# The low part of the attention weights in two GpSimd instructions of 256 columns in a hybrid decoder layer

## The chip, the cores and the metric

One core of a Trainium2 chip. The metric is the time of the kernel on the device in microseconds, median of the runs; less is better. Engines are named as in the profile: PE is TensorE's matmul, PEld its weight load, DVE VectorE, ACT ScalarE, POOL GpSimd, SP the engine that issues the DMAs.

## The reference

A decoder layer on x of 2048 tokens and 1024 channels. The input projection feeds a sparse attention of 8 heads (head dim 64, shared keys and values) and a gated short convolution; then an output projection, a DeepNorm, a SwiGLU FFN of width 2816 and a second DeepNorm. What matters here is the attention: for each query an indexer picks 256 keys, and softmax weights over these multiply the shared values.

```python
logits = jnp.einsum('bqhd,bqkd->bhqk', q_b, kg).astype(jnp.float32) * attn_scale
logits = jnp.where(valid[:, None], logits, NEG_INF)
p = jax.nn.softmax(logits, axis=-1).astype(v.dtype)
return jnp.einsum('bhqk,bqkd->bqhd', p, vg)
```

## The kernel before, in words

The sequence is cut into 16 blocks of 128 queries and 16 tiles of 128 keys. No keys are gathered: a mask `u` per query block holds 0 for a chosen key and a large negative number for the others, and the logits of all keys up to the block get it added. float32 products are made from fp16 pairs: a matrix is split into a high part (its fp16 copy) and a low part (the rest), and three of the four products are summed in PSUM.

The attention goes over the blocks in the order `ORDER`, and in each block over its key tiles, one step per pair of block and key tile, 136 steps in all.

- `weigh` (L881 to L898) makes the weights of a step, in two tiles of 4 heads (128 keys x 512 columns of head and query). Three matmuls make the logits: L888 queries and keys, L889 the mask, L890 minus the row's maximum. ACT takes the exponential into `p32` in float32 (L894) and copies it to fp16 as `ph` (L895). GpSimd subtracts the two, `pr = p32 - ph`, the low part in fp16 (L896). So L896 runs 272 times. `p32` has 5 buffers, `ph` and `pr` have 6 each.
- `values` (L900 to L908) runs `LAG` = 2 steps later. For each of 8 heads it multiplies 128 columns of `ph` with the values' high and low part (L906, L907) and 128 columns of `pr` with the high part (L908), all into one accumulator per block. One `pr` tile serves 4 matmuls of L908, one per 128 columns.
- `finish` (L910 to L923) copies the accumulator to SBUF (L912) and takes squares and sums for the head norm on DVE (L915, L917, L918, L922); `root` (L786 to L798) makes a reciprocal root with ACT and four small DVE operations (L795 to L798).
- `maxima` (L856 to L879) makes the row maxima of later blocks: matmuls of L863, a DVE reduction of each with the mask (L865), and at the end a small product on GpSimd (L878).
- `mix` (L925 onward) is the output projection (L946), residual, norm (L950 to L956) and transposes (L964) of a finished block.
- Beside this, `background` runs the top-k search of the late blocks (11 to 15): counting passes on ACT and DVE (L512, L514) and many small DVE operations on 2 to 12 columns that move the bracket (L517 to L546), then L555 to L564. When they are done, GpSimd, ACT and DVE make the first weights and inputs of the FFN (L215, L216, L1092 to L1111, L1169, L1170).

Which instruction comes when on each engine's queue is not the program's order alone. The kernel is traced in a tile framework, opened as `TileContext(nc, schedule_with_timeline_sim=True)`: it orders the instructions of each engine by their priorities and by a timeline that it works out before the run, and it sets the semaphores. Work on maxima is pulled forward by `tc.high_priority(offset=MXP)` with MXP = 400. On the chip each engine runs its queue in that fixed order.

Of the kernel before, what the change touches and what calls it, by code (L numbers as in the profile page):

```python
# [16 lines left out]
ALU = mybir.AluOpType  # L17
# [10 lines left out]
CH = 512  # L28
# [114 lines left out]
def body(ctx: ExitStack, tc: tile.TileContext, A, out, force=False):  # L143
    nc = tc.nc
    V, S_, G, T = nc.vector, nc.scalar, nc.gpsimd, nc.tensor
# [675 lines left out]
    def attention(pool=None, background=None, at_block=None, at_end=None):  # L821
# [60 lines left out]
        def weigh(b, kt, qst, q2, u):  # L882
            ksl = slice(kt * P, (kt + 1) * P)
            parts = []
            for g in range(2):
                hs = slice(g * 4, g * 4 + 4)
                pl_ = psa.tile([P, CH], F32, tag="l", name="l", bufs=LB)
                T.matmul(pl_, k1T[:, ksl], qst[:, hs], start=True, stop=False)  # L888
                T.matmul(pl_, u[:, ksl], i4, start=False, stop=False)  # L889
                T.matmul(pl_, k2T[:, ksl], q2[:, hs], start=False, stop=True)  # L890
                p32 = aq[0].tile([P, CH], F32, tag="p32", name="p32", bufs=pb_)
                ph = aq[0].tile([P, CH], F16, tag="ph", name="ph", bufs=2 * lag + 2)
                pr = aq[0].tile([P, CH], F16, tag="pr", name="pr", bufs=2 * lag + 2)
                S_.activation(p32, pl_, AF.Exp, scale=DH ** -0.5)  # L894
                S_.activation(ph, p32, AF.Copy)  # L895
                G.tensor_tensor(pr, p32, ph, op=ALU.subtract)  # L896
                parts.append((ph, pr))
            return parts  # L898

# [116 lines left out]
        for i in range(len(steps) + lag):  # L1016
            if i < len(steps):
                p, b, kt = steps[i]
                left = b - kt
                if kt == 0:  # L1020
                    while mixes and mixes[0][2] <= p - keep:
                        advance(mixes.pop(0), 999)
                    if look or p:
                        peak(p + look)
                    urgent(peaks.pop(p), 999)
                    if at_block is not None:
                        at_block(p)
                    mc = ap.tile([P, 4, 2, P], F16, tag="mc", name=f"mc{b}", bufs=keep)
                    dma(mc, m_d[b // 4][:, b % 4])
                    x = ap.tile([P, D], F32, tag="x", name=f"x{b}", bufs=keep)  # L1030
                    dma(x, A["x"][b * P:(b + 1) * P])
                    outs_[p] = x, mc
                tiles_[i] = weigh(b, kt, *held[p])
# [600 lines left out]
```

## Time and profile before

| | |
|---|---|
| median of 3 runs | 2590.02 us (2584.93 to 2590.75) |
| profiled execution, its own time | 2585.36 us |
| its span | 2583.5 us |
| PE busy | 2335.9 us |
| DVE busy | 1835.4 us |
| ACT busy | 1185.9 us |
| POOL busy | 1184.6 us |
| mean granted clock of TensorE | 0.956 |

The profile is one execution; times inside it are microseconds from the start of the span. Durations of single instructions are in nanoseconds. A view by stretches gives each engine's busy time in each stretch; a view by groups puts instructions of one line, operation and shape together with their mean duration and the idle time of the engine in front of them; a view of one line gives its shortest, median and longest duration; the timeline gives start and duration of each instruction.

### The profile page before, as it was taken

What the parts mean: (1) busy time and instruction counts of PE and PEld (TensorE: products, weight loads), DVE (VectorE), ACT (ScalarE), POOL (GpSimd) and SP (SyncE); (2) the same over time, 40 slices, a digit from 0 to 9 for tenths busy, and PEclk for the clock granted to TensorE, in tenths of its full rate; (3) what the DMA queues carried; (4) which work ended last, traced back from release to release, by engine and by line L of the source; (5) the groups of instructions that cost most, each with busy time, mean ns of one, the idle gap of its engine ahead of it and who ended that gap; (6) DMA issues with size and microseconds to landing.
All of it is one profiled execution on the core that took longest, in us unless ns stands there. A gap on an engine that the chain in (4) does not pass through costs nothing. (4 is left out here: it accounts for less than half of the span.)

```text
span 2583.5 us, 38131 instructions
## 1 busy us (share of the span) xinstructions
PE 2335.9 (90%) x13538; PEld 1126.0 (44%) x13538; DVE 1835.4 (71%) x3649; ACT 1185.9 (46%) x2263; POOL 1184.6 (46%) x960
## 2 busy tenths in 40 slices
PE   6799999996878799889969999999999996999998
PEld 3444444443444355445524444444444442444443
DVE  8998999989999877774377676666666687422223
ACT  3687776546766556667643333233323343110000
POOL 3000000004444655786555665565555664855445
PEclk8899999997988899999989999999999997999999
DMA  7321442433131422331233222222223236444443
GB/s 267 130 101 68 144 136 89 161 132 111 59 108 49 145 80 71 106 115 45 84 116 102 90 86 74 76 72 78 86 75 88 87 106 200 149 138 149 131 134 123
DMA packets 213913, 281.69 MB, mean 109 GB/s; under 512 B 15824, under 2 KB 128848, under 8 KB 212944
## 3 DMA queue, kind: packets, MB, share of 16 engines
q1 hardware_dynamic: 213712, 279.17, 33.9%
q8 instruction: 107, 1.75, 0.3%
q14 instruction: 94, 0.77, 0.1%
HBM read 183.20 MB, written 95.91 MB: 108 GB/s over the span
## 5 line engine op out<-in xcount | busy, mean ns | idle before, releaser
L1206 PE MATMUL f<-h,wwg 128*128 128x512 f16 x1800 | 418.8, 383 | 26.5 <-ACT h L1169 19.9
L896 POOL TENSOR_TENSOR pr<-p,ph 128x512 f16<-128x512 f32 x272 | 330.8, 1233 | 218.1 <-ACT ph L895 160.4
L1206 PE MATMUL f<-h,wwu 128*128 128x512 f16 x1800 | 413.5, 379 | 0.0
L1502 PEld LDWEIGHTS <-gi 128*128 128x128 f16 x1848 | 181.5, 99 | 276.1 <-DMA gi<-gg_d 44.8
L1240 POOL TENSOR_TENSOR go<-g,go 128x512 f16<-128x512 f32 x126 | 169.6, 1356 | 275.2 <-ACT go L1239 235.1
L1206 PEld LDWEIGHTS <-wwu 128*128 128x128 f16 x1848 | 180.8, 98 | 234.4 <-issue 17.3
L1206 PEld LDWEIGHTS <-wwg 128*128 128x128 f16 x1848 | 181.8, 99 | 232.0 <-issue 14.1
L1502 PE MATMUL f<-wdo,gi 128*128 128x512 f16 x1032 | 241.9, 387 | 14.9 <-DMA gi<-gg_d 6.9
L865 DVE CUSTOM_DVE_ANT_0 jk<-m,ua 128x512 bf16<-128x512 f32 (+3 forms) x320 | 193.7, 605 | 71.9 <-PE m L863 56.1
L894 ACT ACTIVATE p<-l 128x512 f32<-128x512 f32 x272 | 157.3, 596 | 91.1 <-PE l L890 82.6
L1239 ACT ACTIVATE go<-g 128x512 f16<-128x512 f32 x132 | 82.4, 627 | 230.7 <-issue 82.8
L447 ACT ACTIVATE r<-xs 128x512 f32<-128x512 f32 (+3 forms) x304 | 153.5, 547 | 59.2 <-PE xs L446 15.4
L895 ACT ACTIVATE ph<-p 128x512 f16<-128x512 f32 x272 | 166.1, 632 | 3.9 <-PE o L908 0.8
L1502 PE MATMUL f<-wdr,gi 128*128 128x512 f16 x576 | 136.8, 386 | 16.7 <-DVE g L1213 8.8
L737 PE MATMUL b<-hi,wch 128*128 128x512 f16 x384 | 146.8, 382 | 0.0
L737 PE MATMUL b<-lo,wch 128*128 128x512 f16 x384 | 146.6, 382 | 0.0
L737 PE MATMUL b<-hi,wcl 128*128 128x512 f16 x384 | 146.3, 381 | 0.0
L908 PE MATMUL o<-vst,pr 128*128 128x65 f16 x1088 | 136.1, 197 | 9.3 <-POOL pr L896 9.1
L906 PE MATMUL o<-vst,ph 128*128 128x65 f16 x1088 | 138.7, 195 | 3.1 <-ACT ph L895 2.0
L863 PE MATMUL m<-k1T,qst 128*128 128x512 f16 (+3 forms) x320 | 109.2, 372 | 35.6 <-DVE mp L865 31.5
L907 PE MATMUL o<-vst,ph 128*128 128x64 f16 x1088 | 138.5, 195 | 0.0
L1469 ACT ACTIVATE frs<-fmv,epsw 128x1 f32<-128x1 f32 x16 | 4.7, 295 | 281.7 <-DVE fmv L1466 281.7
(384 smaller groups left out, 5247.2 us busy)
## 6 DMA issues: line engine op xcount, KB each, us to landing
gg_d<-go SPq DMA_DIRECT2D x154, 256.0 KB, 2.6
gi<-gg_d SPq DMA_DIRECT2D x112, 256.0 KB, 3.0
wa<-in_w_ada SPq DMA_DIRECT2D x64, 256.0 KB, 2.9
wg<-in_wg SPq DMA_DIRECT2D x49, 256.0 KB, 2.9
wu<-in_wu SPq DMA_DIRECT2D x49, 256.0 KB, 3.0
wd<-in_wd SPq DMA_DIRECT2D x44, 256.0 KB, 3.0
gi<-gg_d SPq DMA_DIRECT2D x56, 192.0 KB, 2.8
wa<-in_w_ada SPq DMA_DIRECT2D x16, 512.0 KB, 8.6
```

What stands on the lines that cost most here:

```text
L447: S_.activation(r[:, i:i + e], ps[:, 0:e], AF.Relu)
L737: T.matmul(ps, w[:, k, j * P:(j + 1) * P], x[:, k], start=n == 0, stop=n == 3 * KT - 1)
L865: V.tensor_tensor_reduce(jk[:, 0:w], ps[:, 0:w], u[:, j * 512:j * 512 + w], scale=1.0, scalar=-3e38, op0=ALU.add, op1=ALU.max, accum_out=m ...
L894: S_.activation(p32, pl_, AF.Exp, scale=DH ** -0.5)
L895: S_.activation(ph, p32, AF.Copy)
L896: G.tensor_tensor(pr, p32, ph, op=ALU.subtract)
L906: T.matmul(o, lhs, vst[:, kt, 64:129], start=kt == 0 and hh == 0, stop=False)
L907: T.matmul(o[:, 0:64], lhs, vst[:, kt, 0:64], start=False, stop=False)
L908: T.matmul(o, pr[:, hh * P:(hh + 1) * P], vst[:, kt, 64:129], start=False, stop=kt == b and hh == 3)
L1206: T.matmul(ps, w[:, x, k * P:(k + 1) * P], h[:, y, :, k], start=n == 0, stop=n == 11)
L1240: (V if (p, grp) in LASTG else G).tensor_tensor(o[:, :, 1], x4, o[:, :, 0], op=ALU.subtract)
L1502: T.matmul(ps, g[:, p - p0, x], wd_tiles[m, p][:, y], start=p == 0 and n == 0, stop=p == NP - 1 and n == 2)
```

## The change

In `weigh` the one subtraction of 512 columns becomes two of 256 columns, on the same engine, into the two halves of the same tile.

```diff
                 S_.activation(p32, pl_, AF.Exp, scale=DH ** -0.5)
                 S_.activation(ph, p32, AF.Copy)
-                G.tensor_tensor(pr, p32, ph, op=ALU.subtract)
+                for i in range(0, CH, CH // 2):
+                    G.tensor_tensor(pr[:, i:i + CH // 2], p32[:, i:i + CH // 2], ph[:, i:i + CH // 2], op=ALU.subtract)
                 parts.append((ph, pr))
```

## Rows read from the trace of the kernel before

**Rows 1.** The page's first part: engine, busy us, share of the span, instructions.
```profile
PE 2335.9 (90%) x13538; PEld 1126.0 (44%) x13538; DVE 1835.4 (71%) x3649; ACT 1185.9 (46%) x2263; POOL 1184.6 (46%) x960
```
**Rows 2.** Busy time by stretches; columns stand in the first line.
```profile
core 0: us, PE busy (x) PEld busy (x) DVE busy (x) ACT busy (x) POOL busy (x), PEclk, DMA share, GB/s
600.00:900.00 300.00, 231.19 (x1869) 122.92 (x1869) 278.58 (x728) 196.53 (x390) 151.62 (x122) 0.87 0.28 93
900.00:1280.00 380.00, 344.98 (x3467) 198.98 (x3466) 237.29 (x550) 253.00 (x511) 249.91 (x209) 0.98 0.24 82
...
1400.00:2584.00 1184.00, 1132.46 (x5164) 505.64 (x5162) 667.53 (x837) 304.28 (x520) 672.19 (x486) 0.98 0.35 107
```
**Rows 3.** L896: shortest/median/longest ns, first and last start; its group with idle time.
```profile
L896 POOL TENSOR_TENSOR pr<-p,ph x272: 1145/1158/3256, 604.2 to 1272.9; 128x512 f16<-128x512 f32 x136
...
L896 POOL TENSOR_TENSOR pr<-p,ph 128x512 f16<-128x512 f32 x272 | 330.8, 1233 | 218.1 <-ACT ph L895 160.4 <-PE l L890 14.7 <-PE o L908 10.3
```
**Rows 4.** Timelines of POOL and DVE near 660 us: start us, us, instruction.
```profile
659.83 4.51 POOL L896 TENSOR_TENSOR pr<-p,ph 128x512 f16<-128x512 f32 x4
...
660.17 0.84 DVE L518 SCALAR_TENSOR_TENSOR which<-tc,upper 128x6 f32<-128x6 f32 x1
660.93 0.68 DVE L865 CUSTOM_DVE_ANT_0 jk<-m,ua 128x512 bf16<-128x512 f32 x1
...
661.54 0.59 DVE L520 COPY_PREDICATED ends<-which,tc 128x12 f32<-128x12 int32 x1
...
662.67 0.57 DVE L524 TENSOR_TENSOR dd<-ends 128x6 f32<-128x6 f32 x1
```
**Rows 5.** Single lines: shortest/median/longest ns, first and last start us.
```profile
L918 DVE TENSOR_TENSOR ms<-ov x16: 157/166/1240, 622.6 to 1280.0; 128x8 f32<-128x8 f32 x16
...
L745 POOL COPY u<-halo x16: 186/518/1112, 270.0 to 561.2; 128x2 f32<-128x2 f32 x16
...
L878 POOL TENSOR_TENSOR q<-pc,ct x16: 1887/1890/2669, 583.7 to 1207.0; 8x1024 f16<-8x1024 f32 x16
```
**Rows 6.** DVE's groups by shape, 600 to 900 us: busy us, mean ns | idle.
```profile
L915 DVE TENSOR_TENSOR asq<-ov 128x512 f32<-128x512 f32 x8 | 8.0, 994 | 0.0
...
L918 DVE TENSOR_TENSOR ms<-ov 128x8 f32<-128x8 f32 x8 | 4.9, 612 | 0.0
L956 DVE TENSOR_SCALAR z<-z,mvl,rs 128x1024 f32<-128x1024 f32 x6 | 4.8, 804 | 0.1
...
L934 DVE TENSOR_TENSOR al<-m,ah 128x512 f16<-128x512 f32 x6 | 4.1, 683 | 0.0
L797 DVE TENSOR_TENSOR rw<-rw,rv 128x1 f32<-128x1 f32 x6 | 3.9, 658 | 0.0
...
L796 DVE TENSOR_TENSOR rw<-ry 128x8 f32<-128x8 f32 x8 | 2.7, 338 | 0.0
```
**Rows 7.** Instructions on pr by stretches: us, PE, PEld, POOL busy (count).
```profile
600.00:900.00 300.00, 45.57 (x364) 35.56 (x365) 119.90 (x94) 0.87 0.28 93
900.00:1280.00 380.00, 90.49 (x724) 68.75 (x723) 210.94 (x179) 0.98 0.24 82
```
**Rows 8.** Waits, 600 to 900 us, then 900 to 1280: total us, times, longest.
```profile
PEld L908 <- POOL pr L896: 15.8, 19, 2.6
...
PE m L964 <- DVE z L956: 15.8, 8, 2.8
...
PEld L908 <- POOL pr L896: 2.5, 3, 1.9
```
**Rows 9.** DVE's groups by shape, 900 to 1280 us.
```profile
L956 DVE TENSOR_SCALAR z<-z,mvl,rs 128x1024 f32<-128x1024 f32 x9 | 12.8, 1423 | 0.3
...
L797 DVE TENSOR_TENSOR rw<-rw,rv 128x1 f32<-128x1 f32 x9 | 8.2, 907 | 0.2
...
L798 DVE SCALAR_TENSOR_TENSOR rs<-rw,ry 128x1 f32<-128x1 f32 x9 | 6.9, 769 | 0.3
```

## The prediction

> **What bounds the kernel now.** I read the page's busy shares first [rows 1]: PE is busy for 90% of the span, DVE for 71%, POOL for 46%. That is a mean over stages, so the table by stretches came next [rows 2]. From 1400 us to the end PE is busy for 1132 of 1184 us, and L896, the line that changes, no longer runs. L896 runs from 604 to 1273 us [rows 3], so the next thing is to see who sets the pace there. There are two stretches. From 600 to 900 us DVE is busy for 278.6 of 300 us while PE has only 231: DVE is the limit, because the late top-k searches share its queue with the attention. From 900 to 1280 us it is the other way round: PE 345 of 380, DVE 237. POOL is the limit in neither.
>
> Then the line itself [rows 3]. 272 instructions of 512 columns, 1158 ns each in the median, and the mean of 1233 is above it because a few take up to 3256. POOL stands idle for 218 us in front of them, mostly waiting for ACT's fp16 copy.
>
> So at first sight nothing hangs on how POOL cuts this work. The timeline of DVE and POOL side by side shows what does [rows 4]. POOL runs four of these instructions without a break from 659.83 us, that is until 664.34, so they end at about 660.99, 662.11, 663.22 and 664.34. In that time DVE's operation of L518 on 6 columns starts at 660.17 and ends at 661.01; L524 on 6 columns ends at 663.24. Each ends just after one of POOL's ends. Such an operation takes 157 ns at the shortest [rows 5], here it took 840 and 570. The reading: a DVE operation with two inputs in SBUF waits until the POOL instruction that is under way has ended, the whole of it, and then goes ahead of POOL's next one. L865, with one input in PSUM, goes through in 680 ns beside a running POOL instruction and isn't touched.
>
> The Trainium skill, SBUF — State Buffer, section Who interferes with whom, says that the two engines share a port pair, that a DVE instruction with two SBUF inputs contends with a GpSimd instruction that reads SBUF, and that the second to issue blocks fully until the first has finished. The timeline agrees: 840 and 570 ns in place of 157.
>
> **What this costs today.** In the groups of DVE between 600 and 900 us [rows 6] I took each row of a small or two-input operation and multiplied what its mean has over the undisturbed time by its count. Undisturbed is 160 ns for a few columns [rows 5] and 680 for 512 columns (L934, which reads PSUM). L915: 8 x (994 - 680) = 2.5 us; L918: 8 x (612 - 160) = 3.6; L797: 6 x (658 - 160) = 3.0; so on over twenty-one rows, from L915 down to L796 (8 x (338 - 160) = 1.4): 39 us. L896 has 119.9 of POOL's 151.6 us there [rows 2, 7], 79%, so 31 us of DVE's 278.6 are waits behind L896.
>
> **The change, part by part.** Per tile, one POOL instruction of 512 columns goes and two of 256 come. No data moves, no DMA, no tile or buffer is added.
>
> *Price of a half.* The trace has no two-input POOL operation of 256 columns. Nearest rows: a copy of 2 columns takes 186 ns at the shortest [rows 5]. With that as the fixed part, a column costs (1158 - 186) / 512 = 1.90 ns and a half 186 + 486 = 672 ns. Four in a row take 4.51 us [rows 4], so they start (4510 - 1158) / 3 = 1117 ns apart, 41 less than one lasts; halves would start 631 apart. A tile then holds POOL for 1262 ns and not 1117, +145 (13%), and is whole after 1303 ns and not 1158, +145. Its first half is there after 672, 486 ns earlier. The ends: no fixed part, +0 per tile; or the line through L878's 1024 columns in 1890 ns [rows 5], 1.43 ns a column and 426 fixed, a half of 792, starts 751 apart, +34%. I take +145: L896 reads like a plain copy, while L878 has 8 partitions and broadcast inputs.
>
> *POOL.* 272 x 0.145 = 39 us more work. The 218 us of idle time in front of L896 hide it; without that cover it would be 39 us.
>
> *PE.* The matmuls of L908 wait for pr: 15.8 us in 19 waits before 900 us, 2.5 us in 3 after it [rows 8]. Two of the four per tile could start 486 ns earlier, the other two 145 later than today less the time that the first two take. In the first stretch PE isn't the limit, in the second it is 3 waits of 0.15: taken as 0, at most 3 us either way.
>
> *DVE, first stretch.* What DVE loses goes with the share of time in which POOL holds the port and with the length of one hold. The share grows by 1.13, the hold falls to 631 / 1117 = 0.565; the product is 0.64. Of 31 us 20 are left, 11 are saved. At the ends of the price: 0.50 (15.5 saved) and 1.34 x 0.67 = 0.90 (3 saved). DVE is 93% busy there, so I count 0.9 of it: 10 us.
>
> *DVE, second stretch.* PE is the limit, but it waits 15.8 us in 8 waits for DVE's z of L956 [rows 8]. That chain, L796 to L798 and L956, is stretched there [rows 9]: L956 takes 1423 ns against 804 in the first stretch [rows 6], L797 907 and L798 769 against 160. That is 0.6 + 0.75 + 0.6 = 2.0 us per block. L896 has 210.9 of POOL's 249.9 us there [rows 2, 7], so 0.84 x 0.36 x 2.0 = 0.6 us comes off, 8 times 4.8 us; what comes late next is the matmul behind it on PE, so I count half, 2.5 us.
>
> *Sum.* The profiled execution took 2585.4 us; 2585.4 - 10 - 2.5 = 2573. The median of the runs, 2590.0, is 4.6 above that execution, so **2577.5 us**.
>
> A page gives another price for a half. The Trainium skill, GPSIMD Engine Reference, section 3.1, has 4497 ns for a two-input operation of 2048 columns; with the 1158 of this trace that makes an estimate of 2.17 ns a column and only 45 fixed, a half of 601 ns started 560 apart, and 15 us saved in place of 11.
>
> **The rivals.**
>
> *Saved, but not on the path (no change).* In a run of DVE operations that follow closely, the one behind meets the second half and waits again; both halves are then paid as the whole is today, plus 13%: -4 us for DVE in place of +11. For it: L520 and L524 stand close behind L518 in the timeline [rows 4], with 0.68 us of L865 between, longer than a half. Against it: those waits are separated by other operations, and a random arrival waits half of a hold. Halfway between, 2586 to 2590.
>
> *The order laid anew (slower).* The order on each queue is made before the run from a timeline that the planner works out, and two instructions in place of one change its times for pr. Its place is PE's weave of L888 to L890 of later tiles with L908. In the second stretch L908 waits only 3 times. If the new order put it as tightly behind POOL as in the first, 19 of 94 tiles late by 0.83 us [rows 7, 8], then 36 of the 179 would be late by 0.83 + 0.15, 35 us in the stretch that PE limits: 2590 + 35 - 12.5 = 2612. From about 20 such waits on it decides. Nothing in the trace tells how the order will move; against it, the first half is there earlier.
>
> *The port isn't given up between the halves (slower).* Then a DVE operation waits through the pair: share 1.13 and length 1303 / 1158 = 1.13 make 1.27, 8 us more in the first stretch and 3.5 in the second: 2602. Against it: the four in a row [rows 4], where DVE gets in behind each.
>
> By the section of the skill named above, the lock is held for one whole instruction; if a second half that is already queued counted as the first to issue, this rival would come true, and the timeline's four in a row speak against that.
>
> **How the numbers follow.** About 0.3%, 7.8 us, is what a measurement of this kernel can tell from no change: faster is under 2582, slower over 2598. Forecast 0.56 (2561 to 2582); saved off the path 0.25 (2582 to 2597); order laid anew 0.13 (2598 to 2612); port kept 0.06 (2598 to 2602). The bottom of the range is 15.5 us in the first stretch, twice the 2.5 in the second and 5 us for the spread of the runs, with 3 for PE's waits: 2590 - 28.5 = 2561. The top goes into the slower cases until about 0.1 is left: 2602.
>
> **What the profile after would show.** L896 x544 at about 672 ns, starts 631 apart. Among DVE's groups before 900 us L918, L797 and L915 nearer to 400, 400 and 850 ns. DVE's sum for the same work in that stretch down by about 11 us, and L896's last instruction about 12 us earlier than 1273. Halves of 750 ns or more would put the gain at 3 us; DVE waits as long as now would mean the second rival half, or the port kept; more than 20 waits of L908 for pr after 900 us, the order. The forecast is wrong if the last L896 starts no earlier.

## The result, and the profile after

The changed kernel takes **2545.8 us** (median of 4 runs, 2543.0 to 2547.2) beside 2590.4 of the kernel before (4 runs, 2584.9 to 2592.7): ratio 0.9829, 95% interval 0.9811 to 0.9848, or 44.6 us less. The sign was forecast, the size was not: 2577.5 was predicted, and 2561 was the low end of the range.

The first part of the page and the changed line, after:

```profile
PE 2319.4 (91%) x13538; PEld 1119.3 (44%) x13538; DVE 1804.2 (71%) x3649; ACT 1185.0 (47%) x2263; POOL 1230.5 (48%) x1232
...
L897 POOL TENSOR_TENSOR pr<-p,ph 128x256 f16<-128x256 f32 x544 | 379.6, 730 | 140.2 <-ACT ph L895 61.2
```

The view of that line (it is L897 now; every later line moved down by one), and one run of halves in POOL's timeline:

```profile
L897 POOL TENSOR_TENSOR pr<-p,ph x544: 660/672/2713, 602.3 to 1235.0; 128x256 f16<-128x256 f32 x182
...
673.66 3.82 POOL L897 TENSOR_TENSOR pr<-p,ph 128x256 f16<-128x256 f32 x6
```

A half lasts 672 ns, and six follow each other (3820 - 672) / 5 = 630 ns apart, against 1158 and 1117 for a whole one [rows 3, 4]. POOL has 46 us more work in all (1230.5 against 1184.6 [rows 1]) and still 140 us of idle time in front of this line. DVE has 31 us less, for the same 3649 instructions. The last low part starts at 1235.0 and not at 1272.9 [rows 3].

Where the time went shows in a table with the same work in each line: to the end of the 53rd step's last value product, to the end of the attention, to the end. First of before, then after:

```profile
core 0: us, PE busy (x) PEld busy (x) DVE busy (x) ACT busy (x) POOL busy (x), PEclk, DMA share, GB/s
604.00:934.40 330.40, 261.83 (x2167) 140.95 (x2166) 294.77 (x767) 216.42 (x432) 170.29 (x137) 0.88 0.28 93
934.40:1278.50 344.10, 311.44 (x3160) 179.78 (x3158) 215.95 (x494) 230.49 (x465) 230.94 (x192) 0.99 0.23 79
1278.50:2583.50 1305.00, 1225.29 (x5569) 546.69 (x5567) 761.18 (x949) 350.71 (x605) 736.19 (x529) 0.97 0.36 109
```

```profile
604.00:912.70 308.70, 249.17 (x2162) 136.52 (x2161) 275.62 (x766) 214.05 (x428) 187.85 (x243) 0.91 0.29 98
912.70:1237.50 324.80, 304.42 (x3148) 176.54 (x3147) 200.41 (x496) 230.29 (x467) 257.64 (x357) 1.00 0.24 82
1237.50:2542.80 1305.30, 1228.23 (x5582) 547.49 (x5578) 764.13 (x949) 351.21 (x606) 735.87 (x529) 0.97 0.36 110
```

The first stretch is 21.7 us shorter, the second 19.3, the rest as long as before. DVE's busy time falls by 19.2 and 15.5 us with its instructions unchanged: what went is, as the counts under e1 show, waiting inside them. Three groups of DVE from 600 to 900 us, the ones that the prediction named, answer to [rows 6]:

```profile
L916 DVE TENSOR_TENSOR asq<-ov 128x512 f32<-128x512 f32 x8 | 6.1, 765 | 0.0
...
L919 DVE TENSOR_TENSOR ms<-ov 128x8 f32<-128x8 f32 x8 | 3.5, 436 | 0.0
...
L797 DVE TENSOR_TENSOR rw<-rw,rv 128x1 f32<-128x1 f32 x6 | 1.8, 298 | 0.1
```

994, 612 and 658 ns became 765, 436 and 298. And PE's waits from 900 to 1240 us, against [rows 8]:

```profile
PEld L909 <- POOL pr L897: 6.2, 9, 1.8
...
PE m L965 <- DVE z L957: 5.0, 8, 1.5
...
PE o L909 <- POOL pr L897: 3.5, 6, 1.3
```

PE waits 5.0 us for DVE's z where it was 15.8, and somewhat more for `pr`.

### The profile page after: what moved, and what is told of

Read it like the earlier page. It is cut to its first block, busy times and chain, and to the rows that moved or that the text cites. A ratio compares the mean times of both kernels' runs of the same rounds, so it can differ in the third digit from the quotient of the medians.

```text
span 2542.8 us, 38397 instructions
## 1 busy us (share of the span) xinstructions
PE 2319.4 (91%) x13538; PEld 1119.3 (44%) x13538; DVE 1804.2 (71%) x3649; ACT 1185.0 (47%) x2263; POOL 1230.5 (48%) x1232
## 4 chain that ended last, share of the span: by engine, by line
PE 35%; POOL 6%; DMA 4%; DVE 3%; issue 2%; ACT 0%; SPq 0%; DVEq 0%; POOLq 0%
PE f L1207 30%; PE f L1503 5%; DMA x<-xn_d 2%; POOL z L1480 1%; DMA gi<-gg_d 1%; POOL x L1491 1%; POOL x L1490 1%; POOL z L1547 1%; POOL z L1548 1%; DMA wd<-in_wd 1%; DVE wdo L216 0%; DVE h L1171 0%; DVE z L1536 0%; POOL wd L1112 0%; POOL yd L1105 0%
## 5 line engine op out<-in xcount | busy, mean ns | idle before, releaser
L897 POOL TENSOR_TENSOR pr<-p,ph 128x256 f16<-128x256 f32 x544 | 379.6, 730 | 140.2 <-ACT ph L895 61.2
L909 PE MATMUL o<-vst,pr 128*128 128x65 f16 x1088 | 140.4, 196 | 14.4 <-POOL pr L897 13.7
L908 PE MATMUL o<-vst,ph 128*128 128x64 f16 x1088 | 141.5, 194 | 0.0
```

The lines of the kernel that those rows point to most:

```text
L897: G.tensor_tensor(pr[:, i:i + CH // 2], p32[:, i:i + CH // 2], ph[:, i:i + CH // 2], op=ALU.subtract)
L908: T.matmul(o[:, 0:64], lhs, vst[:, kt, 0:64], start=False, stop=False)
L909: T.matmul(o, pr[:, hh * P:(hh + 1) * P], vst[:, kt, 64:129], start=False, stop=kt == b and hh == 3)
```

## The experiments

Theories to be told apart. **Holds**: POOL holds what the two engines share (the prediction's "port") for shorter times, so DVE's small operations wait less. **Order**: two instructions in place of one change the planned times, and with them the order of all queues; at 2695 of PE's 13538 places and 751 of DVE's 3649 the changed kernel's queue holds another instruction than that of before (another line, tile or shape; counted in the traces). **Early half**: two of the four products on a `pr` tile can start before the other half is made. And for the prediction's sizes: which stretch pays.

To hold the order still, the low part was cut after the order had been laid: L896's instruction is replaced in the finished queue by parts of it, of which the first keeps the wait and the last gives the signal (in e2, as in the changed kernel, both parts signal). Every other queue is then that of before, instruction by instruction (or that of the changed kernel, where the experiment starts from that one). In the traces of e1 and e10 every place of PE's, DVE's and ACT's queues holds the same instruction as before, in those of e2 and e3 the same as in the changed kernel.

| run | order of | cut, columns | median us (range) | ratio [95%] |
|---|---|---|---|---|
| e1 | before | 256+256 | 2556.8 (2554.8 to 2560.2) | 0.9879 [0.9862, 0.9896] |
| e10 | before | 510+2 | 2571.9 (2568.3 to 2572.2) | 0.9930 [0.9912, 0.9947] |
| e4 | before | 4 x 128 | 2579.8 (2577.1 to 2587.8) | 0.9974 [0.9962, 0.9986] |
| e7 | before | 256+256 from step 54 on | 2573.0 (2567.5 to 2575.2) | 0.9931 [0.9913, 0.9950] |
| e8 | before | 256+256 up to step 53 | 2573.0 (2570.4 to 2576.4) | 0.9936 [0.9919, 0.9953] |
| e2 | changed kernel | 510+2 | 2558.4 (2557.4 to 2562.3) | 0.9893 [0.9874, 0.9911] |
| e3 | changed kernel | 256+256, PE waits for the second half | 2546.1 (2544.9 to 2547.6) | 0.9842 [0.9825, 0.9859] |
| e9 | changed kernel | 256+256, and L878 in two | 2542.5 (2541.9 to 2545.3) | 0.9823 [0.9806, 0.9840] |
| e5 | its own, a third | 510+2 | 2578.6 (2574.6 to 2580.0) | 0.9957 [0.9941, 0.9974] |
| e6 | that of e5 | 256+256, PE waits for the second half | 2562.1 (2560.2 to 2563.5) | 0.9892 [0.9876, 0.9909] |
| e11 | a fourth, laid for 384+128 | 256+256, PE waits for the second half | 2549.9 (2549.7 to 2555.5) | 0.9849 [0.9833, 0.9865] |
| e12 | its own, a fifth | 176+176+160 | 2557.2 (2555.0 to 2560.6) | 0.9875 [0.9858, 0.9891] |

Medians of 4 runs (9 for e4). e1 to e4 ran beside a before of 2588.4, e5 to e8 of 2590.6, e9 to e12 of 2588.6. An interval of a ratio is some 4.5 us to either side, and differences between rows are to be read with that.

### Halves in the order of before (e1)

```diff
+at = [x.name for x in block.instructions].index(i.name)
+n = CH // 2
+block.instructions[at:at + 1] = [_part(i, j * n, n, j == 0, j == 2 - 1, ...) for j in range(2)]
```

The arguments of `_part` are the instruction, the first column, the number of columns, whether it waits and whether it signals.

> The order of every engine's queue is that of the kernel before. Each 512-column instruction of L896 is cut in two only after the order is fixed; the first half takes the wait, the second alone signals, so PE gets nothing earlier. Theory 'short hold' (DVE waits less behind POOL, and the stages shorten with it): most of the 44 us, 2545 to 2560, DVE's waits behind pr at 0.63 of before (about 25 us before 900 us where before has 40). Theory 'new order' (the order laid out anew brings it): the short hold gives the first stretch's 15 us at most, 2575 to 2590. Theory 'early half' (PE starts on the first half): 2588 to 2595, the second half is 145 ns later for everyone.

Measured: 31.6 us less than before, in the order of before and without an early signal. By the same stretches, in the profiled executions (2585.4 us before and 2560.2 here, so 25.2 apart and not 31.6):

```profile
604.00:921.00 317.00, 256.97 (x2167) 137.46 (x2166) 280.56 (x767) 214.97 (x429) 188.91 (x245) 0.88 0.29 96
921.00:1252.40 331.40, 310.50 (x3159) 179.11 (x3158) 203.40 (x494) 231.23 (x467) 258.45 (x357) 0.99 0.24 83
```

13.4 us less in the first, 12.7 in the second: most of the gain comes with the cut alone. How much of that is the shorter hold, and how much the mere second instruction, e10 tells. What DVE lost behind L896 I counted over the whole trace (its operations more than 80 ns over their shortest that start while a POOL instruction on `pr` runs). Before it is 44.1 us in 65 waits in the first stretch and 39.2 in 51 in the second; in e1 31.4 in 76 and 25.1 in 63. More waits, each shorter. The sums fall by 12.7 and 14.1 us, and the stretches by 13.4 and 12.7: **here a microsecond less of DVE's waiting is about a microsecond less of the span, in the stretch that PE limits as well.** (In e10's second stretch it is half of that.)

How it gets there in the second stretch: PE's waits from 930 to 1280 us, before and then e1, whose own waits for `pr` are longer.

```profile
PE m L964 <- DVE z L956: 13.5, 7, 2.8
...
PEld L908 <- POOL pr L896: 2.5, 3, 1.9
```

```profile
PEld L908 <- POOL pr L896: 6.6, 11, 2.0
...
PE m L964 <- DVE z L956: 3.9, 6, 1.3
```

PE's wait for z is 9.6 us shorter, its weight load's wait for `pr` 4.1 longer. The chain in front of it, DVE's groups from 930 to 1240 us, before and then e1 (busy us, mean ns | idle):

```profile
L956 DVE TENSOR_SCALAR z<-z,mvl,rs 128x1024 f32<-128x1024 f32 x7 | 9.7, 1380 | 0.2
...
L797 DVE TENSOR_TENSOR rw<-rw,rv 128x1 f32<-128x1 f32 x7 | 6.1, 868 | 0.2
...
L798 DVE SCALAR_TENSOR_TENSOR rs<-rw,ry 128x1 f32<-128x1 f32 x7 | 5.7, 811 | 0.2
...
L796 DVE TENSOR_TENSOR rw<-ry 128x1 f32<-128x1 f32 x7 | 4.2, 594 | 1.6 <-ACT ry L794 1.6
```

```profile
L956 DVE TENSOR_SCALAR z<-z,mvl,rs 128x1024 f32<-128x1024 f32 x7 | 8.1, 1157 | 0.2
...
L798 DVE SCALAR_TENSOR_TENSOR rs<-rw,ry 128x1 f32<-128x1 f32 x8 | 4.3, 533 | 0.2
...
L797 DVE TENSOR_TENSOR rw<-rw,rv 128x1 f32<-128x1 f32 x8 | 3.7, 467 | 0.2
...
L796 DVE TENSOR_TENSOR rw<-ry 128x1 f32<-128x1 f32 x8 | 2.3, 288 | 3.2 <-ACT ry L794 3.2
```

The four means add up to 3653 ns before and 2445 in e1: 1.21 us less per block, 8.5 us over 7 blocks.

The stretch behind the attention is as long in e1 as before (1306.0 and 1305.0 us), so the gain reaches the end. The chain of waits shows the same: it runs back from the last instruction to the long row of FFN products that follows the attention. Before, e1, after:

```profile
1362.12 706.85 PE f L1206 x3263
```

```profile
1336.93 705.97 PE f L1206 x3263
```

```profile
1321.53 751.41 PE f L1207 x3467
```

It begins 25.2 us earlier in e1 and 40.6 earlier after. (After counts a longer run, as its chain is followed through more of the same products.)

### One stretch at a time (e7, e8)

```diff
 for k, (block, i) in enumerate(list(_low(nc))):
+    if k >= 106:
```

This is e7; e8 has `k < 106`. k counts the tiles, two for each step, so 106 is the first of step 54.

> The order of before, halves put in after the order is fixed, but only for the 166 tiles from the 54th step on (the stretch that PE limits, after about 930 us). Theory 'short hold on the chain to z': 12 to 18 us faster than before, 2570 to 2577, PE's waits for z there from 13.5 to about 4 us and nothing else changed. If the stretch gains only because the first one ended otherwise: 2583 to 2590.

> The order of before, halves only for the 106 tiles of the first 53 steps (the stretch that DVE limits). Theory 'short hold': 11 to 16 us faster than before, 2572 to 2578, and the second stretch as long as before (344 us). With the run on the second stretch it should sum to the 31 us of both; if not, one depends on the other.

Measured: 17.6 and 17.5 us less than the 2590.6 beside them; together 35, against 31.6 for both at once (e1), equal within the intervals. The second stretch of e7, from 931.1 us on, is 11.2 us shorter than before, and its PE waits for z are down to 4.4 us:

```profile
931.10:1264.00 332.90, 313.10 (x3162) 179.89 (x3160) 202.37 (x494) 231.30 (x467) 257.74 (x356) 0.98 0.24 83
```

e8 is 13.7 us shorter in the first stretch, and its second, left as it was, is as long as before (343.6 and 344.1 us):

```profile
604.00:920.70 316.70, 255.77 (x2160) 137.25 (x2159) 281.11 (x767) 214.08 (x428) 186.03 (x240) 0.88 0.29 95
920.70:1264.30 343.60, 309.62 (x3160) 179.13 (x3158) 217.44 (x494) 230.98 (x468) 232.00 (x193) 0.99 0.23 79
```

So the stretch that the prediction gave 2.5 us is worth about as much as the one that it gave 10. How closely a single trace tells a stretch shows in e7's first one: nothing is cut there, and it is 3.3 us shorter than before (604 to 931.1).

### The early half (e3)

In the changed kernel's finished queues every wait of PE for the count that a first half brings (`up` holds these counts) is moved on to the second half's (one line of the edit):

```diff
+w = [w.__replace__(wait_value=w.wait_value + 1) if w.id == sem and w.wait_value in up else w for w in s.on_wait]
```

> The changed kernel, but every wait of PE for a first half is a wait for the second half. Theory 'early half': loses a good part of the 44 us, 2560 to 2590. Theories 'short hold' and 'new order': 2544 to 2552, a few us at most, as PE waited for pr 8 us in all after 900 us.

Measured: 2546.1, the changed kernel 2545.8; against the before beside each, 42.3 and 44.6 us less. In the changed kernel's trace the first product on a tile starts before the second half is done for 52 of 272 tiles, in e3's for none. That PE can take the first half early brings nothing that can be measured.

### A second instruction without shorter holds (e2, e10)

The tile is cut into 510 and 2 columns: the long hold stays, DVE gets one more chance per tile. e2 does it in the order of the changed kernel, e10 in that of before.

```diff
-block.instructions[at:at + 1] = [_part(i, j * n, n, j == 0, j == 2 - 1, ...) for j in range(2)]
+block.instructions[at:at + 1] = [_part(i, 0, CH - 2, True, False, ...), _part(i, CH - 2, 2, False, True)]
```

> The order of every queue is that of the changed kernel, but the two instructions of a tile have 510 and 2 columns in place of 256 and 256, so a hold is as long as before and POOL's sum about that of the changed kernel. Theory 'short hold': back to 2585 to 2600, DVE's waits behind pr back at 40 us before 900 us. Theory 'new order': 2545 to 2565. Theory 'early half': 2585 to 2595.

> The control: the order of before, 510 and 2 columns put in after the order is fixed. POOL has about as much to do as with halves, and the hold is as long as before. Theory 'short hold': 2588 to 2596. If it comes near the 2557 of the halves in the same order, it is the second instruction and not the length of the hold that helps DVE in.

e2 was meant as "the new order, whole holds". At 2558.4 it is 12.3 us slower than e3, and 30 faster than before, which would make the order worth 30. But 30.0 and e1's 31.6 are 61.6, and the change brings 42.3 (e3): they don't add up unless the 2 columns themselves do something. e10 is the control for that: the order of before, and still 16.7 us less. So e2's 30.0 are 16.7 of the 2-column instruction and about 13.5 of the order (e10 to e2). This is a miss of theory 'short hold' as it was written, which gave e10 no gain: of e1's 31.6 us, 16.7 come with a second instruction even of 2 columns, and 15.1 more with the even cut, which alone shortens the hold.

How 2 columns can help shows in e10's timelines from 662 us: first POOL, in three overlapping pieces (the second is the 2-column part from 663.48 and the long one from 663.64 together), then DVE.

```profile
662.37 1.15 POOL L896 TENSOR_TENSOR pr<-p,ph 128x510 f16<-128x510 f32 x1
...
663.48 1.31 POOL L896 TENSOR_TENSOR pr<-p,ph 128x2 f16<-128x2 f32 x2
...
663.64 1.14 POOL L896 TENSOR_TENSOR pr<-p,ph 128x510 f16<-128x510 f32 x1
```

```profile
662.39 1.15 DVE L797 TENSOR_TENSOR rw<-rw,rv 128x8 f32<-128x8 f32 x1
663.46 0.15 DVE L536 SCALAR_TENSOR_TENSOR f<-ends,a 128x3 f32<-128x3 f32 x1
663.57 0.17 DVE L798 SCALAR_TENSOR_TENSOR ms<-rw,ry 128x8 f32<-128x8 f32 x1
663.66 1.16 DVE L537 TENSOR_SCALAR f<-f 128x3 f32<-128x3 f32 x1
```

L797 comes 20 ns after a long part has begun and lasts until it ends, 1.15 us on 8 columns. L536 and L798 then go through in 0.15 and 0.17 beside the 2-column part. L537 comes 20 ns after the next long part and pays in full again. My reading: DVE's operations come in close rows, and what they pay goes with the number of POOL instructions they meet and with the length of each; another short instruction lets a row get on by one or two operations, where otherwise the next whole tile would have begun. One row illustrates this and doesn't prove it, but DVE's waits behind L896 fit: 37.7 and 29.2 us in e10, between before (44.1, 39.2) and e1 (31.4, 25.1). That is 16.4 us less waiting in all, for 16.7 us less time. By stretches it goes one to one less well:

```profile
604.00:925.00 321.00, 254.47 (x2160) 135.79 (x2160) 287.51 (x767) 214.41 (x429) 187.41 (x241) 0.89 0.28 93
925.00:1263.90 338.90, 312.19 (x3159) 179.59 (x3158) 206.50 (x494) 230.83 (x466) 258.82 (x356) 0.98 0.24 80
```

The first stretch is 9.4 us shorter for 6.4 us less waiting, the second 5.2 for 10.0; PE's wait for z is still 9.2 us there.

### The cut in a third order (e5, e6), and a fourth (e11)

```diff
-for i in range(0, CH, CH // 2):
-    G.tensor_tensor(pr[:, i:i + CH // 2], p32[:, i:i + CH // 2], ph[:, i:i + CH // 2], op=ALU.subtract)
+for i, j in ((0, CH - 2), (CH - 2, CH)):
+    G.tensor_tensor(pr[:, i:j], p32[:, i:j], ph[:, i:j], op=ALU.subtract)
```

That is e5. e6 is e5 with both instructions set to 256 columns in the finished queue, and with e3's late signal; e11 is the same from a source that cuts at 384.

> The changed kernel's source with cuts of 510 and 2 columns, and the order laid out for that: a third order, neither that of before nor that of the changed kernel, with holds as long as before. Theory 'any other order' (the order before is a poor one, so a new one brings some 30 us): 2550 to 2570. Theory 'this order' (the changed kernel's order happens to be a good one): 2580 to 2600.

> The third order, that of the 510 and 2 columns, with halves of 256 put in after the order is fixed, PE waiting for the second half. Against the run with 510 and 2 columns in the same order, theory 'short hold' expects 15 to 32 us less, as in the order of before (31) and in the changed kernel's (13); no gain would make those a matter of the order.

> Halves of 256 in a fourth order, the one laid out for 384 and 128 columns. Halves in the orders so far: 2557 (that of before), 2562 (that of 510 and 2), 2546 (the changed kernel's). Theory 'the order is chance': between 2545 and 2565; below 2545 or over 2570 it moves more than so far seen.

With 510+2 in the source the planner lays a third order. At the same cut it is 6.6 us slower than that of before (e10 to e5), and with halves 5.3 slower (e1 to e6), where the changed kernel's order is 13.5 and 10.7 faster. The fourth is 6.9 faster with halves (e1 to e11). Taken as gains over the before that ran beside each, the 6.6 and 5.3 are 4.7 and 3.2, so that the third order is slower is not clear of noise. The even cut brings 16.5 in the third order, 12.3 in the changed kernel's, 15.1 in that of before. So cut and order add up nearly independently, and the orders seen lie between some 13 us faster than that of before and a few slower. That the changed kernel got a good one is luck of the draw as far as these runs tell. The order of before wasn't simply a poor one: theory 'any other order' expected 2550 to 2570 for e5, and it took 2578.6.

What in that order brings the 11 us stays open. In the second stretch PE's idle time is nearly the same as in e1 (20.4 and 20.9 us), and its busy time is 6 us less (304.4 against 310.5) for nearly as many instructions. The granted clock there is 1.00 after and 0.99 in e1, which can be a part of it; e3, at 0.99 too, is busy for 307.0 of 326.0 us (912 to 1238). In the first DVE is 5.0 us less busy and the stretch 8.3 shorter. DVE's waits behind the low part are 52.6 us after and 50.4 in e3, against 56.5 in e1, which would cover some 5 us of the 11; but e2 has as many as e10 (67.6 and 66.9) and is still 13.5 faster. Nor is it the granted clock in the first stretch: e3 has 0.89 there and the changed kernel 0.91, at the same time.

### Finer cuts (e4, e12)

```diff
-n = CH // 2
-block.instructions[at:at + 1] = [_part(i, j * n, n, j == 0, j == 2 - 1, ...) for j in range(2)]
+n = CH // 4
+block.instructions[at:at + 1] = [_part(i, j * n, n, j == 0, j == 4 - 1, ...) for j in range(4)]
```

e12 cuts in the source, at 176 and 352, and takes the order that comes of it.

> As the first, with four instructions of 128 columns, about 429 ns each and 390 apart; POOL gets 0.44 us more work per tile. Theory 'short hold': DVE's waits behind pr fall to about half of before (1.40 x 0.35 = 0.49), 2540 to 2555, unless POOL becomes late in the second stretch (its share goes from 66% to over 85%), which would show as waits of PE for pr and 2555 to 2570. Theory 'new order': 2575 to 2600.

> The changed kernel with three instructions of 176, 176 and 160 columns and its own order: about 505 ns each, 1.40 us per tile. Theory 'short hold': DVE's waits behind pr a little below those of halves, 0.53 of before against 0.64; but POOL is closer to its limit in the second stretch, so 2540 to 2555, the order adding 10 us either way.

Quarters give most of the gain back: 2579.8, 23 us slower than halves in the same order, and slower than either range expected of theory 'short hold' (2540 to 2555, or 2555 to 2570). DVE's waits behind L896 do fall further, to 23.7 and 19.0 us. But a quarter lasts 426 ns, so a tile holds POOL for some 1.5 us in place of 1.3, and PE now waits for `pr`. The line, the second stretch and PE's waits in it:

```profile
L896 POOL TENSOR_TENSOR pr<-p,ph x1088: 415/426/2468, 601.7 to 1266.0; 128x128 f16<-128x128 f32 x182
```

```profile
921.30:1270.40 349.10, 317.21 (x3159) 179.46 (x3158) 192.18 (x494) 231.75 (x466) 307.61 (x688) 0.98 0.23 79
```

```profile
PEld L908 <- POOL pr L896: 30.4, 46, 1.8
...
PE o L908 <- POOL pr L896: 15.9, 29, 1.7
```

POOL is busy for 307.6 of 349.1 us (88%), and the stretch is 5 us longer than before the change, while the first (604 to 921.3) keeps its gain of 13.1: in the second POOL has become the one that PE waits for. Thirds, in an order of their own, are 11 us slower than the changed kernel; their DVE waits are 28.0 and 32.1 us, so they don't beat halves, but order and cut are not told apart there.

### The other long hold (e9)

The changed kernel, with L878's product of 8 x 1024 in two instructions of 4 heads each, in the finished queue:

```diff
+block.instructions[at:at + 1] = [part(0, True, False, ...), part(1, False, True, i.name)]
```

> The changed kernel and its order, with the product of L878 (8 partitions, 1024 columns, 1.89 us, 16 times) cut in two of 512 after the order is fixed. In the changed kernel DVE waits some 6 to 8 us behind L878 in the first stretch. Theory 'short hold': 2 to 5 us faster than the changed kernel, 2541 to 2544; 2546 if the fixed cost eats it.

Measured: 2542.5 against 2545.8 of the changed kernel; the ranges overlap (2541.9 to 2545.3 and 2543.0 to 2547.2), and against the before beside each it is 46.1 and 44.6 us less. It is the fastest of all kernels here, but not shown apart from the change.

## Why the prediction was right and wrong

**The mechanism was right in the main.** DVE waits behind a POOL instruction under way and, in nearly all cases, not behind the next one as well; with shorter instructions the waits are shorter, and the rivals that deny it fell. Two inputs in SBUF are not needed for it, though: L537, with one tile as input, takes 1.16 us in e10's timeline and waits like the others. *Port not given up between the halves*: waits would have grown to 1.27, they fell to 0.71 and 0.64 in e1. *Saved, but not on the path*: the operation behind does meet the second half, as that rival had it (116 waits before, 139 in e1), but then it waits for one half (the longest wait in e1 is some 0.57 us, before 1.03): 83.3 us in sum became 56.5.

**The rule for the size was right by luck in part.** "What DVE loses goes with the share of time in which POOL holds the port and with the length of one hold": by this rule 510 and 2 columns, with a larger share and the same long hold, gain nothing. e10 gained 16.7 us, its waits fell to 0.80 of before. What a second turn does for a close row of operations is no term of the rule, and yet it is about half of what the cut brings; that 0.64 lies near the 0.71 and 0.64 measured doesn't show the rule.

**The price of a half was right**: 672 ns and 630 apart, forecast 672 and 631. POOL's work rose by 46 us and not 39, as some halves are themselves stretched (mean 730), and was hidden as said.

**PE and the early half**: taken as 0, measured as 0 (e3).

**The first stretch**: 10 us forecast, 13.4 in e1. The factor 0.64 came out as 0.71, on a larger sum than 31 us: 44.1, since the stretch goes on to 934 us and all waits behind L896 were counted (some 40 up to 900 us).

**The step that failed is the one on DVE in the second stretch**: "0.6 us comes off, 8 times 4.8 us; what comes late next is the matmul behind it on PE, so I count half, 2.5 us". It measured 11 to 13 us (e7, e1). Three things in it were too small. The chain lost 1.21 us per block and not 0.6: I took 0.84 of its stretch as due to L896 and 0.36 of that off, which leaves a factor of 0.70. By the four means, less the 160 and 804 ns that the prediction called undisturbed (1284 together), 2369 ns became 1161, a factor of 0.49. L796, 594 ns before and 288 in e1, wasn't in my sum at all; that a close row of operations gains more than single ones at random is my reading of the rest. The half that I struck off for a matmul that comes late next was too much: PE's wait for z went from 13.5 to 3.9 us, and its weight load's wait for `pr` grew by 4.1. And the rest of DVE's waits in that stretch, 39.2 us in sum with the chain's, were not counted because PE is the limit there; they fell by 14.1 us in e1 and the stretch by 12.7.

**The order** was a rival with one sign only, slower, from 20 waits of L908 on. After has 9 such waits of the weight load and 6 of the matmul from 900 to 1240 us, so the mechanism named for it didn't come. The order itself did change, and gave 10.7 us the other way (e1 to e3). Nothing in the trace of before could tell the sign, so it belonged in the range on both sides. That it came out as a gain is luck. 31.6 and 10.7 make the 42.3 of e3, of which 12.5 were forecast; the cut alone would have ended below the range too (e1, 2556.8).

## What to carry to other kernels

Where DVE and GpSimd run side by side, look at DVE's operations on a few columns: where they take a microsecond in place of 0.16, GpSimd's long instructions are a cost of DVE, whoever is the bound, and cutting them is worth it until GpSimd's fixed part makes it the one that others wait for (here halves of 512 gained 31.6 us, quarters 8.6). Count such waits as a possible gain also in a stretch that another engine limits, if that engine waits for the end of the stretched chain: with tiles cut in two, half (e10) to nearly all (e1) of what they fell by there came off the time. A change of one instruction lays the planner's order anew; hold the order still, by changing the finished queue, before you credit the change with what the order gave.

## What the runs showed of the hardware

An instruction of 2 columns on POOL gave 16.7 us by itself (e10), though every long hold stayed; DVE's waits behind L896 fell from 83.3 to 66.9 us with it. The Trainium skill, SBUF — State Buffer, section Who interferes with whom, says that whoever issues first has the shared ports for the whole instruction and the other blocks until then; e10's L797, 1.15 us behind a part of 1.15, agrees. What these runs add is that DVE mostly gets in when POOL's instruction ends, even when POOL's next one is queued: before, 115 of the 116 counted waits ended with the POOL instruction under way. The other one (L1170 at 1105.7 us, 1.71 us long) began within 50 ns of that end and waited for the next instruction as well; in e1 six did, each begun within 100 ns of the end of a half.

POOL's fixed part is large. Of L896 in e10:

```profile
L896 POOL TENSOR_TENSOR pr<-p,ph 128x510 f16<-128x510 f32 x272 | 327.6, 1204 | 164.1 <-ACT ph L895 85.7 <-issue 66.3 <-POOL pr L896 6.0
...
L896 POOL TENSOR_TENSOR pr<-p,ph 128x2 f16<-128x2 f32 x272 | 70.2, 258 | 0.0
```

2 columns take 184 ns at the shortest, 128 take 426, 256 take 672 and 512 take 1158: some 180 ns fixed and 1.9 a column, as the copy of 2 columns [rows 5] had it. The Trainium skill, GPSIMD Engine Reference, section 3.1, led to an estimate of 45 ns fixed and 601 for a half; the measured 672 decides against it.
